# Value products of attention in longer runs, and gate and up by slices of the input, in a two-layer hybrid trunk

## The chip, the cores and the metric

The kernel runs on one core of one Trainium2 chip. The time is that of one launch on the device, in microseconds (us): 2272.66 us, the median of three runs that lie between 2272.47 and 2272.93 us. The profile is one further execution of the same program, recorded by the hardware profiler.

## The reference

One sequence of 512 tokens with 1024 features passes through two decoder layers. Each layer has three sub-layers, a feed-forward network (FFN), a token mixer and a second FFN, and each sub-layer is wrapped in the same way:

```python
def sandwich(x, fn, pre_g, post_g, shift, scale, gate, res_w):
    hn = rmsnorm(x, pre_g) * (1 + scale[:, None, :]) + shift[:, None, :]
    y = rmsnorm(fn(hn), post_g)
    return x + res_w * gate[:, None, :] * y

def swiglu(h, w_gate, w_up, w_down):          # FFN, inner width 2816
    return (jax.nn.silu(h @ w_gate) * (h @ w_up)) @ w_down
```

The mixer of layer 0 is multi-head latent attention (MLA): 16 heads, causal, in blocks of 128 queries. The core of it:

```python
s = jnp.einsum('bhqd,bhkd->bhqk', qi, kt) * scale     # masked: key position <= query position
p = jax.nn.softmax(s, axis=-1)
return jnp.einsum('bhqk,bhkd->bhqd', p, vt)           # the value products
```

The mixer of layer 1 is dilated attention (DIL): 16 heads of 64, each in three groups with dilation 1, 4 and 16 and a window, with a relative-position bias. The groups' outputs are added with weights from a softmax over their log-sum-exps:

```python
proj = (h @ w_in).reshape(B, S, N_GROUPS, 3, DIL_HEADS, DIL_HEAD_DIM)     # q, k, v of three groups
...
alpha = jax.nn.softmax(jnp.stack(lses, axis=0), axis=0)
o = jnp.sum(alpha[..., None] * jnp.stack(outs, axis=0), axis=0)
return o.reshape(B, S, DIL_WIDTH) @ w_o
```

All of it is in float32.

## The kernel before, in words

**Products.** Every product with a weight is three TensorE matmuls (`mm3`, lines 143, 144 and 145 of the profile): weight and input are split into a high and a low part, and high by high, high by low and low by high are added up in one PSUM bank. The high part of a weight is made by ScalarE (ACT, line 128, tile `whi`, 128x1024), the low part by VectorE (DVE, line 130, tile `wlo`, in two halves). Both come from a ring: six slots for `whi`, six for `wlo`, five for the raw weights that SyncE's queue (SP) loads. A slot is free when the last matmul that reads it has ended. PSUM has eight banks: four with the tag `mm` for products and scores, taken in turn, and four with the tag `aux` for transposes and value products.

**Stages.** The six sub-layers run one after the other: FFN, MLA, FFN, FFN, DIL, FFN. In the profile MLA's attention lies at about 447 to 590 us and DIL's at about 1396 to 1880 us, the FFNs before, between and behind.

**FFN.** Its 22 slices of 128 inner columns are in four groups of 5, 6, 5 and 6. `head` computes one slice: 24 matmuls for gate into one bank, 24 for up into a second (`gate_up_mm`), then `silu` on ACT (L567), the product on DVE (L569) and its split (L570, L572). After a group's last slice `down` multiplies the group with its slices of w_down.

**MLA.** `attend(c, i)` handles a pair of heads c and a block i of queries in three steps: `score` (L862), `turn`, which transposes the softmax's output on TensorE (L890) and copies it to SBUF, and `weigh`, the value products (L904). A value product uses 64 columns of the array (the profile's 128*64), one head in the upper and one in the lower half. A `Pipe` with a lag of 2 sets score of block i beside turn of an earlier and weigh of a still earlier block; products for the next heads (`BESIDE`) are put in between.

**DIL.** `rest` goes through 7 pairs p; in each it computes the nine projections of pair p+1 in the order (0, 1, 3, 4, 6, 7, 2, 5, 8), place n = 0 to 8. `tile` is one projection: 24 matmuls into one `mm` bank, which ACT then copies out (L1055) in one piece, or in four where group 2 needs another order of tokens (n = 4 and n = 5). Beside the projections stand `scores(p, n)` at n = 0 to 3 (L1090, two `mm` banks each, 64 rows of the array), `exps(p)` at n = 4 (48 exponentials on ACT, L1155), and `mix(p, step)`: `turn` (transposes, L1210, and copies) and `weigh` (value products, L1235, 128*64 again). Steps 0, 1 and 2 stand at n = 6, 7 and 8, steps 3 and 4 in the next pair at n = 0 and 1. The transposes at L1065 are those of the value projections.

**Order.** Apart from SP at the start and TensorE and DVE in DIL's last part, no order is written out: a list scheduler takes the program in the order of the code with its own costs and gives each engine a fixed list of instructions, which the engine works off in that order. So an edit of the code on TensorE can move instructions on the other engines.

Of the kernel before, what the change touches and what calls it, by code (L numbers as in the profile page):

```python
# [520 lines left out]
class Ffn:  # L521
# [19 lines left out]
    def gate_up_mm(self, ft, lo, hi, banks, ks):  # L541
        t = self.t
        if ft not in self.w:
            self.gate_up_load(ft)
        for g in range(2):
            for k in ks:
                t.mm3(
                    banks[g],
                    [x[:, k, :] for x in self.w[ft][g]],
                    [x[k][:, lo:hi] for x in t.h],  # L550
                    k == 0,
                    k == KT - 1,
                )
# [25 lines left out]
    def products(self, b, q, i, d, js):  # L579
        m = GROUPS[q][1]  # L580
        for j in js:
            self.t.mm3(
                b,
                [x[j][:, i * P : (i + 1) * P] for x in self.g[q]],
                [x[:, d * SEQ : (d + 1) * SEQ] for x in self.wd[q][j]],
                j == 0,
                j == m - 1,
            )
# [24 lines left out]
    def rest(self):  # L613
        t = self.t
        last = len(GROUPS) - 1
        for q, (at, n) in enumerate(GROUPS):
            if q == last - 1:
                t.gates(self)
            for ft in range(max(at, START if t.first is self else HEAD), at + n):
                self.head(ft, 0, SEQ)  # L620
                t.pump(3 if t.first is self else 2)
            for i in range(TT if q < last else 0):
                self.down(q, i)
# [76 lines left out]
class Mla(Mixer):  # L700
# [148 lines left out]
    def attend(self, c, i, pipe):  # L849
        t, nc = self.t, self.t.nc  # L850
        sc = 96.0**-0.5
        if i == 0:
            self.st = t.tmp.tile([P, 4, 6], F32, tag="st", name="st", bufs=3), {}
        st, box = self.st
        q, k = self.q[c], self.k[c]

        def score(i):
            n = (i + 1) * P
            box[i] = []
            for e in range(2):  # L860
                s = t.bank()[:, :n]
                nc.tensor.matmul(s, q[e][0:96, i * P : n], k[e][0:96, :n], start=True, stop=True)  # L862
                p = (t.t("u", UB) if i % 2 else t.t("sq", SB))[:, :n]
                nm, z = st[:, i, e : e + 1], st[:, i, 2 + e : 3 + e]
                nc.vector.tensor_tensor_reduce(
                    p, s, self.mask[:, SEQ - n :], -sc, 3e38, ALU.add, ALU.min, accum_out=nm
                )
                nc.scalar.activation(p, p, AF.Exp, bias=nm, scale=-1.0, accum_out=z)
                box[i].append(p)
            r = st[:, i, 4:6]  # L870
            nc.vector.reciprocal(r, st[:, i, 2:4])
            p = box[i]
            nc.vector.tensor_scalar(p[0], p[0], r[:, 0:1], None, ALU.mult)
            nc.scalar.activation(p[1], p[1], AF.Copy, scale=r[:, 1:2])

        def turn(i):
            n = (i + 1) * P
            tag = "gg" if i % 2 else "silu"
            ps = [t.bank("aux")]
            ys = [t.t(tag)]  # L880
            if i < 2:
                ps.append(ps[0][:, n:])
                ys.append(ys[0][:, n:])
            else:
                ps.append(t.bank("aux"))
                ys.append(t.t(tag))
            for e in range(2):
                for j in range(i + 1):
                    r = slice(j * P, (j + 1) * P)
                    nc.tensor.transpose(ps[e][:, r], box[i][e][:, r], t.ident)  # L890
            if i < 2:
                nc.vector.tensor_copy(ys[0][:, : 2 * n], ps[0][:, : 2 * n])
            else:
                nc.scalar.activation(ys[0][:, :n], ps[0][:, :n], AF.Copy)
                nc.vector.tensor_copy(ys[1][:, :n], ps[1][:, :n])
            box[i] = ys

        def weigh(i):
            if i == 0:
                box["o"] = t.bank("aux")  # L900
            for j in range(i + 1):
                for e in range(2):
                    h = 2 * c + e
                    nc.tensor.matmul(  # L904
                        box["o"][64 * e : 64 * e + 64, i * P : (i + 1) * P],
                        self.v[j, h // 8][:, (h % 8) * 64 : (h % 8) * 64 + 64],
                        box[i][e][:, j * P : (j + 1) * P],
                        start=i == j == 0,
                        stop=i == j == 3,
                        skip_group_check=True,  # L910
                    )
            if i == 3:
                self.put_o(box["o"])

        pipe.push(i, score, turn, weigh)

    def rest(self):
# [25 lines left out]
class Dil(Mixer):  # L943
# [302 lines left out]
            self.of.append(x)  # L1246

    def mix(self, p, step):
        if step < 4:
            self.turn(p, step)  # L1250
        if step:
            self.weigh(p, step - 1)

    def rest(self):
        t = self.t
        t.gates(self)
        self.of = []
        self.tables()
        for u in self.ORDER[6:]:
            self.tile(0, u, 0, SEQ)  # L1260
        for p in range(7):
            for n, u in enumerate(self.ORDER):
                if n < 4:
                    self.scores(p, n)
                if n < 2 and p:
                    self.mix(p - 1, 3 + n)
                if n == 4:
                    self.exps(p)
                if n >= 6:
                    self.mix(p, n - 6)  # L1270
                if p == 6 and n == 8:
                    self.scores(7, 0)
                self.tile(p + 1, u, 0, SEQ)
        self.later()
        self.scores(7, 1)
        for x in self.of[:PART]:
            self.put_o(x)
        self.mix(6, 3)
        t.new_y()
        for j in range(PART):  # L1280
            self.out_weights(j)
        self.scores(7, 2)
        self.mix(6, 4)
        self.scores(7, 3)
        for x in self.of[PART:]:
            self.put_o(x)
        self.exps(7)
        order = (2, 0, 1, 3)
        with t.tc.manual_schedule(engines={PE, DVE}):
            for n in range(6):  # L1290
                self.part(n)
            for n, step in enumerate(order):
                self.turn(7, step)
                if n:
                    self.weigh(7, order[n - 1], order[0], order[-1])
                if n in (0, 1):
                    self.part(6 + n)
            self.norm_out(self.pairs[7])
            self.weigh(7, order[-1], order[0], order[-1])
        self.put_o(self.of[-1])  # L1300
# [115 lines left out]
```

## Time and profile before

| | |
|---|---|
| median of three runs | 2272.66 us (2272.47 to 2272.93) |
| profiled execution | 2273.08 us |
| its span, first to last instruction | 2271.3 us |
| TensorE (PE) busy | 2240.5 us, 99% |
| VectorE (DVE) busy | 1203.6 us, 53% |
| ScalarE (ACT) busy | 861.3 us, 38% |
| GpSimd (POOL) busy | 105.2 us, 5% |
| granted TensorE clock, mean | 0.999 |

A line of the profile names engine, source line, operation, and the tiles as out<-in, with buffer numbers left out. In a timeline a row is a start, a duration, and a count (x8) of like instructions in succession. Matmuls overlap: one begins before the other ends, so the distance of two starts, not the duration, says what a matmul takes of TensorE's time. A bracket at a row's end is the time for which the engine stood idle before it, with what ended this wait. Value products and scores stand in the trace with two records for each matmul of the code, so x16 there is x8 in a list of the order.

### The profile page before, as it was taken

What the parts mean: (1) busy time and instruction counts of PE and PEld (TensorE: products, weight loads), DVE (VectorE), ACT (ScalarE), POOL (GpSimd) and SP (SyncE); (2) the same over time, 40 slices, a digit from 0 to 9 for tenths busy, and PEclk for the clock granted to TensorE, in tenths of its full rate; (3) what the DMA queues carried; (4) which work ended last, traced back from release to release, by engine and by line L of the source; (5) the groups of instructions that cost most, each with busy time, mean ns of one, the idle gap of its engine ahead of it and who ended that gap; (6) DMA issues with size and microseconds to landing.
All of it is one profiled execution on the core that took longest, in us unless ns stands there. A gap on an engine that the chain in (4) does not pass through costs nothing. (4 is left out here: it accounts for less than half of the span.)

```text
span 2271.3 us, 30190 instructions
## 1 busy us (share of the span) xinstructions
PE 2240.5 (99%) x11422; PEld 1851.4 (82%) x11422; DVE 1203.6 (53%) x2712; ACT 861.3 (38%) x1752; POOL 105.2 (5%) x143
## 2 busy tenths in 40 slices
PE   7999999999999999999999999999999999999998
PEld 5888888877898888898888888778878878888887
DVE  7666566677655366474554473334434367243344
ACT  4422135577633132353222352444344346332232
POOL 0000001210110000020000010000000002000000
PEclk9999999999999999999999999999999999999999
DMA  8575662311255365344653523333333332243231
GB/s 307 163 249 180 187 232 68 100 48 57 76 171 180 93 213 173 106 140 127 191 174 114 156 93 105 80 96 87 81 93 87 89 79 80 75 130 100 76 111 38
DMA packets 121224, 284.04 MB, mean 125 GB/s; under 512 B 44130, under 2 KB 48501, under 8 KB 121078
## 3 DMA queue, kind: packets, MB, share of 16 engines
q1 hardware_dynamic: 121078, 282.11, 40.8%
q8 instruction: 89, 1.46, 0.3%
q14 instruction: 57, 0.47, 0.1%
HBM read 279.67 MB, written 2.39 MB: 124 GB/s over the span
## 5 line engine op out<-in xcount | busy, mean ns | idle before, releaser
L143 PE MATMUL mm<-s,whi 128*128 128x512 f32 (+1 forms) x2116 | 796.9, 377 | 3.5 <-ACT whi L128 2.4
L144 PE MATMUL mm<-s,whi 128*128 128x512 f32 (+1 forms) x2116 | 790.9, 374 | 0.0
L145 PE MATMUL mm<-s,wlo 128*128 128x512 f32 (+1 forms) x2116 | 790.5, 374 | 0.0
L128 ACT ACTIVATE whi<-raw 128x1024 fp32r<-128x1024 f32 (+1 forms) x356 | 369.7, 1053 | 962.2 <-PE mm L144 446.6
L130 DVE TENSOR_TENSOR wlo<-raw,whi 128x512 fp32r<-128x512 f32 (+1 forms) x712 | 465.6, 693 | 397.8 <-ACT whi L128 393.8
L143 PEld LDWEIGHTS mm<-s,whi 128*128 128x128 f32 x2116 | 398.7, 188 | 83.4 <-issue 7.0
L145 PEld LDWEIGHTS mm<-s,wlo 128*128 128x128 f32 x2116 | 398.7, 188 | 70.9
L144 PEld LDWEIGHTS mm<-s,whi 128*128 128x128 f32 x2116 | 398.9, 188 | 68.1
L143 PE MATMUL mm<-whi,s 128*128 128x512 f32 x848 | 332.4, 392 | 1.8 <-ACT s L694 1.1
L144 PE MATMUL mm<-wlo,s 128*128 128x512 f32 x848 | 330.4, 390 | 0.0
L145 PE MATMUL mm<-whi,s 128*128 128x512 f32 x848 | 330.1, 390 | 0.0
L165 DVE CUSTOM_DVE_ANT_0 raw<-raw,cs 128x1024 f32<-128x1024 f32 x130 | 159.9, 1234 | 117.7 <-DMA raw<-w_mod 117.2
L143 PEld LDWEIGHTS mm<-whi,s 128*128 128x128 f32 x848 | 159.2, 188 | 36.3 <-issue 2.5
L145 PEld LDWEIGHTS mm<-whi,s 128*128 128x128 f32 x848 | 159.2, 188 | 33.4 <-issue 0.3
L144 PEld LDWEIGHTS mm<-wlo,s 128*128 128x128 f32 x848 | 159.3, 188 | 32.6 <-issue 0.3
L569 DVE TENSOR_TENSOR gg<-silu,mm 128x512 f32<-128x512 f32 (+1 forms) x95 | 60.3, 635 | 171.5 <-PE mm L145 168.3
L459 DVE TENSOR_TENSOR s<-mm,s 128x512 f32<-128x512 f32 x112 | 76.5, 689 | 125.8 <-PE mm L145 125.6
L318 POOL TENSOR_TENSOR mv<-mv,mhalf 128x1 f32<-128x1 f32 x48 | 36.0, 752 | 1498.0 <-DVE mv L317 1495.5
L570 ACT ACTIVATE s<-gg 128x512 fp32r<-128x512 f32 (+1 forms) x97 | 57.4, 591 | 62.0 <-DVE gg L569 62.0
L567 ACT ACTIVATE silu<-mm 128x512 f32<-128x512 f32 (+1 forms) x95 | 51.5, 543 | 31.9 <-PE mm L145 31.9
L1055 ACT ACTIVATE s<-mm 128x512 f32<-128x512 f32 (+3 forms) x156 | 46.2, 373 | 34.8 <-PE mm L145 34.8
L463 ACT ACTIVATE s<-mm 128x512 f32<-128x512 f32 x40 | 23.8, 595 | 85.8 <-PE mm L145 85.5
(168 smaller groups left out, 1737.3 us busy)
## 6 DMA issues: line engine op xcount, KB each, us to landing
raw<-w_gu SPq DMA_DIRECT2D x168, 512.0 KB, 4.3
raw<-w_mod SPq DMA_DIRECT2D x130, 512.0 KB, 4.8
raw<-w_down SPq DMA_DIRECT2D x88, 512.0 KB, 4.3
raw<-dil_in SPq DMA_DIRECT2D x70, 512.0 KB, 3.6
s<-w_mod SPq DMA_DIRECT2D x28, 256.0 KB, 6.3
raw<-w_gu SPq DMA_DIRECT2D x16, 256.0 KB, 3.6
raw<-mla_o SPq DMA_DIRECT2D x8, 512.0 KB, 3.7
raw<-dil_o SPq DMA_DIRECT2D x8, 512.0 KB, 3.6
```

Source lines behind the costliest of these rows:

```text
L128: self.nc.scalar.activation(hi, raw, AF.Copy)
L130: self.nc.vector.tensor_tensor(lo[:, r], raw[:, r], f(hi[:, r]), ALU.subtract)
L143: mm(out, w[0], m[0], start=first, stop=False)
L144: mm(out, w[0], m[1], start=False, stop=False)
L145: mm(out, w[1], m[0], start=False, stop=last)
L165: nc.vector.tensor_tensor_reduce(raw, raw, self.cs, 1.0, 0.0, ALU.mult, ALU.add, accum_out=t[:, 0:1])
L318: nc.gpsimd.tensor_tensor(v[:, 1:2], v[:, 0:1], self.mhalf[:, 0:1], ALU.pow)
L459: nc.vector.tensor_tensor(y, b, y, ALU.add)
L567: nc.scalar.activation(s, banks[0], AF.Silu)
L569: nc.vector.tensor_tensor(v, s, banks[1], ALU.mult)
L570: nc.scalar.activation(ghi, v, AF.Copy)
L1055: nc.scalar.activation(out, src, AF.Copy)
```

## The change

Three edits. `gate_up_mm` loops over the input's slices outside and over gate and up inside, so that its matmuls alternate between the two banks. In MLA the value products of blocks 0 and 1, and of blocks 2 and 3, are set together. In DIL `weigh` of steps 0 and 1 is issued at step 2 and that of steps 2 and 3 at step 4, ahead of the transposes of that step, and the two calls of `mix` for the former pair stand before `scores(p, 0)` and behind `scores(p, 1)`.

```diff
@@ Ffn.gate_up_mm
-        for g in range(2):
-            for k in ks:
+        for k in ks:
+            for g in range(2):
                 t.mm3(
                     banks[g],
@@ Mla.attend
         def weigh(i):
             if i == 0:
                 box["o"] = t.bank("aux")
+            elif i % 2:
+                for q in (i - 1, i):
+                    products(q)
+            if i == 3:
+                self.put_o(box["o"])
+
+        def products(i):
             for j in range(i + 1):
                 for e in range(2):
                     h = 2 * c + e
...
-            if i == 3:
-                self.put_o(box["o"])
@@ Dil.mix
     def mix(self, p, step):
+        if step in (2, 4):
+            for n in (step - 2, step - 1):
+                self.weigh(p, n)
         if step < 4:
             self.turn(p, step)
-        if step:
-            self.weigh(p, step - 1)
@@ Dil.rest
             for n, u in enumerate(self.ORDER):
+                if n == 0 and p:
+                    self.mix(p - 1, 3)
                 if n < 4:
                     self.scores(p, n)
-                if n < 2 and p:
-                    self.mix(p - 1, 3 + n)
+                if n == 1 and p:
+                    self.mix(p - 1, 4)
```

With it the lines move: L904 becomes L911, and in DIL L1055 becomes L1060, L1065 L1070, L1090 L1095, L1155 L1160, L1210 L1215 and L1235 L1240.

**TensorE in MLA.** The rows are TensorE's, from the transposes of one block to the next product; L862 are scores, L890 transposes, `aux<-silu,s` and `aux<-gg,s` the value products of even and odd blocks. Before:

```order
L862 MATMUL mm<-s 128x384 x2
L890 MATMUL aux<-ident,sq 128x128 x2
L904 MATMUL aux<-gg,s 64x128 x8
L143 MATMUL mm<-s,whi 128x512
...
L862 MATMUL mm<-s 128x512 x2
L890 MATMUL aux<-ident,u 128x128 x4
L904 MATMUL aux<-silu,s 64x128 x2
L143 MATMUL mm<-whi,s 128x512
```

After the change:

```order
L862 MATMUL mm<-s 128x384 x2
L890 MATMUL aux<-ident,sq 128x128 x2
L911 MATMUL aux<-silu,s 64x128 x6
L911 MATMUL aux<-gg,s 64x128 x8
L143 MATMUL mm<-whi,s 128x512
...
L862 MATMUL mm<-s 128x512 x2
L890 MATMUL aux<-ident,u 128x128 x4
L143 MATMUL mm<-whi,s 128x512
```

Two runs of value products are now one. Over MLA there were 32 separate runs and there are 18.

**TensorE in DIL, from place n = 7 to n = 8 of a pair.** Here with the buffers' numbers: `mm_14061` before and `mm_14056` after is the bank of the projection at n = 7, `mm_14120` that at n = 8. Before:

```order
L145 MATMUL mm_14061<-s_11065,wlo_14056 128x512
L1235 MATMUL aux_14048<-gg_14036,s_13544 64x256
L1235 MATMUL aux_14048<-gg_14042,s_13544 64x256
L1235 MATMUL aux_14048<-gg_14036,s_13544 64x128
L1235 MATMUL aux_14048<-gg_14042,s_13544 64x128
L143 MATMUL mm_14120<-s_11058,whi_14114 128x512
L144 MATMUL mm_14120<-s_11066,whi_14114 128x512
```

After the change:

```order
L145 MATMUL mm_14056<-s_11065,wlo_14051 128x512
L143 MATMUL mm_14120<-s_11058,whi_14114 128x512
L144 MATMUL mm_14120<-s_11066,whi_14114 128x512
L145 MATMUL mm_14120<-s_11058,wlo_14115 128x512
L143 MATMUL mm_14120<-s_11059,whi_14114 128x512
L144 MATMUL mm_14120<-s_11067,whi_14114 128x512
L1070 MATMUL aux_14082<-ident_75,s_14009 128x128 x4
L1240 MATMUL aux_14089<-silu_13988,s_13539 64x256
```

The value products between the two projections are gone; they stand behind the next transposes of a value projection. In all DIL has 32 runs of value products before and 18 after.

**ScalarE in DIL, the same pair.** The rows begin with the last exponentials of the pair. `mm_13922` is the bank of n = 4, `mm_13959` that of n = 5, `mm_14010` of n = 6; the four `whi` slots named are those of later projections. Before:

```order
L1155 ACTIVATE u_13804,dz_13625<-u_13804,y4_13830 128x128 x4
L128 ACTIVATE whi_14317<-raw_14315 128x1024
L128 ACTIVATE whi_14389<-raw_14387 128x1024
L1055 ACTIVATE s_13921<-mm_13922 128x128 x4
L1055 ACTIVATE s_13958<-mm_13959 128x128 x4
L1055 ACTIVATE s_14009<-mm_14010 128x512
L1055 ACTIVATE s_14060<-mm_14061 128x512
L128 ACTIVATE whi_14464<-raw_14462 128x1024
```

After the change:

```order
L1160 ACTIVATE u_13804,dz_13629<-u_13804,y4_13830 128x128 x4
L128 ACTIVATE whi_14317<-raw_14315 128x1024
L128 ACTIVATE whi_14389<-raw_14387 128x1024
L128 ACTIVATE whi_14464<-raw_14462 128x1024
L1060 ACTIVATE s_13921<-mm_13922 128x128 x4
L1060 ACTIVATE s_13958<-mm_13959 128x128 x4
L1060 ACTIVATE s_14009<-mm_14010 128x512
L1060 ACTIVATE s_14055<-mm_14056 128x512
```

The third conversion (`whi_14464`) stands ahead of ten copies instead of behind them. It is so in pairs p = 1 to 6; in pair p = 0 three conversions stand ahead of the copies before and after the change.

## Rows read from the trace of the kernel before

**Rows 1.** The page's first part: busy time, share of the span and instructions.

```profile
PE 2240.5 (99%) x11422; PEld 1851.4 (82%) x11422; DVE 1203.6 (53%) x2712; ACT 861.3 (38%) x1752; POOL 105.2 (5%) x143
```

**Rows 2.** Waits of TensorE: line, releaser, us in total, times, longest.

```profile
PE mm L143 <- ACT s L306: 3.8, 6, 1.2
```

**Rows 3.** Timeline of TensorE in MLA: start, duration, line, tiles, count.

```profile
500.88 1.09 PE L904 MATMUL aux<-gg,s 128*64 128x128 f32 x16
501.90 0.50 PE L143 MATMUL mm<-s,whi 128*128 128x512 f32 x1
...
505.79 0.60 PE L890 MATMUL aux<-ident,u 128*128 128x128 f32 x4
506.32 0.44 PE L904 MATMUL aux<-silu,s 128*64 128x128 f32 x4
506.69 0.50 PE L143 MATMUL mm<-whi,s 128*128 128x512 f32 x1
507.03 0.40 PE L144 MATMUL mm<-wlo,s 128*128 128x512 f32 x1
```

**Rows 4.** Timeline of TensorE late in DIL, transposes directly ahead of products.

```profile
1855.22 1.04 PE L1210 MATMUL aux<-ident,u 128*128 128x128 f32 x8
...
1856.32 0.40 PE L144 MATMUL mm<-wlo,s 128*128 128x512 f32 x1
```

**Rows 5.** Timeline of TensorE in DIL, pair p = 1, n = 6 to 8.

```profile
1508.22 0.82 PE L1210 MATMUL aux<-ident,sq 128*128 128x128 f32 x6
1508.97 1.08 PE L1235 MATMUL aux<-silu,s 128*64 128x256 f32 x8
...
1510.33 0.40 PE L144 MATMUL mm<-s,whi 128*128 128x512 f32 x1
...
1515.37 0.39 PE L145 MATMUL mm<-s,wlo 128*128 128x512 f32 x1
1515.69 0.87 PE L1235 MATMUL aux<-gg,s 128*64 128x256 f32 x8
1516.49 0.50 PE L143 MATMUL mm<-s,whi 128*128 128x512 f32 x1
1516.83 0.40 PE L144 MATMUL mm<-s,whi 128*128 128x512 f32 x1
```

**Rows 6.** Timeline of TensorE, value products directly behind scores.

```profile
1524.80 1.09 PE L1235 MATMUL aux<-silu,s 128*64 128x128 f32 x16
1525.83 0.50 PE L143 MATMUL mm<-s,whi 128*128 128x512 f32 x1
```

**Rows 7.** Timeline of TensorE in DIL, pair p = 0, n = 7 to 8.

```profile
1452.12 0.39 PE L145 MATMUL mm<-s,wlo 128*128 128x512 f32 x1
1452.44 0.87 PE L1235 MATMUL aux<-gg,s 128*64 128x256 f32 x8
1454.16 0.50 PE L143 MATMUL mm<-s,whi 128*128 128x512 f32 x1 [0.85 <-ACT s L1055]
1454.49 0.39 PE L144 MATMUL mm<-s,whi 128*128 128x512 f32 x1
```

**Rows 8.** Timeline of ScalarE in the same stretch, pair p = 0.

```profile
1452.38 1.06 ACT L128 ACTIVATE whi<-raw 128x1024 fp32r<-128x1024 f32 x1 [6.34 <-PE mm L144]
1453.34 2.42 ACT L1055 ACTIVATE s<-mm 128x128 f32<-128x128 f32 x10
```

**Rows 9.** Timeline of ScalarE in pair p = 1.

```profile
1509.20 1.93 ACT L1055 ACTIVATE s<-mm 128x128 f32<-128x128 f32 x9
...
1516.35 1.05 ACT L128 ACTIVATE whi<-raw 128x1024 fp32r<-128x1024 f32 x1
```

**Rows 10.** Timeline of VectorE where an FFN's group of slices begins.

```profile
1159.74 2.50 DVE L130 TENSOR_TENSOR wlo<-raw,whi 128x512 fp32r<-128x512 f32 x4 [1.08 <-ACT whi L128]
```

**Rows 11.** Timeline of TensorE at the same place.

```profile
1161.85 0.39 PE L143 MATMUL mm<-s,whi 128*128 128x512 f32 x1
...
1162.98 0.39 PE L145 MATMUL mm<-s,wlo 128*128 128x512 f32 x1
```

## The prediction

> **What bounds the kernel now.** I read the page's busy times first: TensorE is busy for 99% of the span, VectorE for 53%, ScalarE for 38% [rows 1]. So time is saved only where TensorE's own list of instructions becomes shorter, and lost wherever TensorE is made to wait. Next came its waits: where an FFN takes over its input, six waits for ACT's L306 add up to 3.8 us [rows 2]; none of the list is for a value product's operand. Then the timeline of TensorE at the places that the change touches, looking at the distance of starts: five steps of a 512-column product from 1161.85 to 1162.98 us are 1.13 us, 0.226 us each [rows 11]. Last the same stretches on ACT, since TensorE in DIL depends on ACT's copies for free banks.
>
> **What a run of value products costs beside its own work.** In MLA four transposes, four value products and a product follow one another: from the first transpose (505.79) to the second product (507.03) it is 1.24 us [rows 3]. Without the value products, eight transposes take 1.10 us to the same point, 1855.22 to 1856.32 [rows 4]. A transpose takes 0.11 us: six need 0.75 (1508.22 to 1508.97) [rows 5], four 0.53 (505.79 to 506.32) [rows 3], and two more make 0.22. So four transposes without value products take 1.10 - 0.44 = 0.66 us. The value products' own work: 16 take 1.02 us to the next product (500.88 to 501.90), four take 0.37 (506.32 to 506.69), so 0.65/12 = 0.054 us each and 0.22 for four [rows 3]. What is left is 1.24 - 0.66 - 0.22 = 0.36 us for one separate run: 0.15 of it between its first record and the product behind, 0.1 in the slower first step of that product (0.34 instead of 0.23), the rest at its entry.
>
> *A page against these rows.* The Trainium skill, TensorE: Matmul & The Clock Gate, section Step-by-step: what each phase is for, says that one matmul's drain runs beside the next one's fill, so that matmuls in succession are spaced by their columns alone. By that a run's ends would cost nothing and merging runs would save nothing. The trace differs here: 0.34 us behind a run against 0.226 us elsewhere.
>
> **MLA.** 32 separate runs become 18: 14 x 0.36 = 5.0 us saved. The work of the products is the same. What a merged run costs is not shown for a run of two tiles; the lower bound of the saving is the 0.15 us inside alone, 14 x 0.15 = 2.1 us, the upper one 0.36 each. I take the upper one, since entry and exit both go with the run. The even block's value products now come later, so their `silu` buffer comes free later, and the copies of the next block wait on it on DVE; behind them are transposes and scores of a next block, which the pipe's lag of two keeps off TensorE's path. I put nothing for it. If that cover were gone, TensorE would lose up to the length of a run of 16 for each pair of heads, 8 x 1.02 = 8 us [rows 3]; only the range's upper part holds some of that.
>
> **DIL, the runs.** In each of seven pairs the runs of steps 0 and 1 become one: one overhead less, 0.36 us. The rows agree: from the transposes at 1508.22 to the second product at 1510.33 it is 2.11 us, of which six transposes and two products are 1.10 - 0.22 = 0.88; from the last product ahead (1515.37) to the second one behind (1516.83) 1.46, of which two steps are 0.46; 2.23 us in all for both runs [rows 5]. Steps 2 and 3 stand next to score runs in both versions. There 16 value products take 1.03 us until the product (1524.80 to 1525.83), of which 16 x 0.054 = 0.87 is work; 0.16 is saved when two such runs become one [rows 6]. Together 0.52 x 7 = 3.6 us. Bounds: 0.15 and 0.72 for both, 1.1 to 5.0 us.
>
> **DIL, ACT's list.** This is where I expect the gain to go. Moving the value products from n = 7 to n = 8 changes the scheduler's list for ACT: in pairs 1 to 6 a third weight conversion (L128) stands ahead of the ten copies (L1055) that free the banks of n = 4 to 7. That conversion's slot is the one that the projection at n = 7 reads, six conversions earlier, so it cannot begin before the last matmul of n = 7 that reads it. And the first matmul at n = 8 needs the bank of n = 4, the fourth back, whose copies stand behind that conversion. So TensorE stands still for a conversion and four copies.
>
> The trace shows this very order once, in pair 0. ACT waits 6.34 us for a product L144, begins the conversion at 1452.38, and the copies at 1453.34 [rows 8]. TensorE's last product of n = 7 begins at 1452.12, so n = 8 could begin at 1452.12 + 0.23 = 1452.35; it begins at 1454.16, with 0.85 us of it shown as a wait for L1055, and its next step takes 0.33 instead of 0.23 [rows 7]. Part of it is covered there by value products. Without them the loss is 1454.16 - 1452.35 + 0.10 = 1.91 us. In pair 1, where only two conversions stand ahead, the copies begin at 1509.20 [rows 9], 7.3 us before n = 8 needs its bank at 1516.49, and the eight products take 0.80 us, with no wait [rows 5]; the third conversion comes at 1516.35, when the copies are done [rows 9].
>
> After the change all seven pairs have the order of pair 0, and the value products no longer stand in the gap: 7 x 1.91 = 13.4 us. Pair 0 lost already 1454.16 - 1452.44 - 0.80 = 0.92 us [rows 5, 7]. The change adds 13.4 - 0.9 = 12.5 us. Behind the waiting conversion on ACT stand the ten copies, 2.42 us in all [rows 8]; who waits for these is TensorE at n = 8, and five products later the value projection's transposes. The timeline of pair 0 shows no bracket ahead of these, so I add none. Bounds: below, the shown wait alone, 7 x 0.85 - 0.85 = 5.1 us, or nothing at all if the bank were free; above, a wait for all ten copies, 7 x (0.03 + 0.96 + 2.42 + 0.10) - 0.9 = 23.7 us.
>
> **FFN.** The matmuls are the same in number and form, and gate and up use two banks as before; at 0.226 us a step it makes no difference which comes first. What changes is when up's weight is needed: after three matmuls of a slice, not after 24. Where a group begins, DVE makes four low halves from 1159.74 in 2.50 us, so the third, up's first, is there by 1161.6 [rows 10]; TensorE starts the slice at 1161.85 and needs that half five steps later, at 1162.98 [rows 11]. 1.3 us are left, so nothing is lost. In return silu and the product for a slice come both at its end; the next slice's 48 matmuls (10.8 us at 0.226) hide them. Where an FFN takes over its input, TensorE waits for the input's slices and not for the order of gate and up [rows 2]; both orders end at the arrival of the last one. I put 0, with 2 us either way for these places: about half of the 3.8 us.
>
> **The sum.** -5.0 - 3.6 + 12.5 = +3.9 us. The profiled execution took 2273.08 us, 1.8 us beyond its span, and is 0.4 us above the median; the same execution after the change would take 2277.0 us, and the median 2272.66 + 3.9 = about 2276.5 us.
>
> **Rivals.**
> *ACT does not hold TensorE* (faster). If the slot or the bank were free in time in pairs 1 to 6, as before, only the runs count: 2272.66 - 5.0 - 3.6 = 2264.1 us. For it: before the change six of seven pairs show no wait. Against it: pair 0, where the same three conversions stand ahead and the wait is there. Chance 0.14.
> *Half of it holds.* If TensorE loses only the 0.95 us that pair 0 shows as a wait and slow step: 7 x 0.95 - 0.92 = 5.7, so 2272.66 - 8.6 + 5.7 = 2269.8 us. For it: something else of TensorE's list might stand in the gap, as value products did. Against it: the list shows only the products of n = 8 there. Chance 0.08.
> *The FFN pays for up's weight* (slower). One mechanism: at the twelve places where a group follows another within an FFN, up's first low half comes too late. It decides once more than 1.3 us of other work stands ahead of that half on DVE; three further halves of 0.62 us (1.88) would leave a wait of 0.5 us, 12 x 0.5 = 6 us, and 2282.5 us with the rest. For it: the weights of w_down are made by the same engine in the same stretch. Against it: the margin of 1.3 us [rows 10, 11]. Chance 0.09.
> *Merging saves nothing* (slower): the runs' ends cost TensorE no time that it could use otherwise, and only the waits count, 2272.66 + 12.5 = 2285.2 us. Against it: the 0.36 us in rows 3 and 4. Chance 0.07. The rule cited above, of the Trainium skill, TensorE: Matmul & The Clock Gate, section Step-by-step: what each phase is for, would have it so.
>
> **How the numbers follow.** My forecast has 0.62, with a range of its own of 2273 to 2280 us. A measurement of this kernel can tell about 0.2%, 4.5 us, from no change, so the limit lies at 2277.2 us, close above the forecast; of its 0.62 I put 0.38 below the limit and 0.24 above. Faster: 0.14, the first rival. Same: 0.38 + 0.08 = 0.46. Slower: 0.24 + 0.09 + 0.07 = 0.40. For 8 in 10 the range reaches from 2265, near the first rival, to 2283 us, past the FFN's.
>
> **What would show it.** Right: waits of TensorE for the moved copies (L1060) at n = 8 of every pair, of about 1.8 us each and 12 to 13 us in all; ACT's third conversion beginning at the end of n = 7 in each pair; MLA's attention shorter by about 5 us; DIL longer by about 9; the FFNs equal within 2. Wrong: no such wait, or one of under a microsecond; value products in long runs whose next product still takes as much per run; a new wait for `wlo` (L130) in an FFN, or for a copy in MLA.

## The result, and the profile after

The changed kernel takes 2280.99 us (median of six runs, 2278.15 to 2284.72) where the kernel before took 2273.32 us in its six (2272.47 to 2275.56). The ratio is 1.0032, with a 95% interval of 1.0022 to 1.0042: about 7.3 us longer, where I had forecast 3.9 us. The profiled execution of after took 2280.28 us, its span is 2278.5 us against 2271.3.

TensorE is busy for as long as before (2239.4 us against 2240.5); it waits more. Its waits after (line, releaser, us in total, times, longest):

```profile
PE mm L143 <- ACT s L1060: 9.9, 6, 1.6
PE mm L377 <- DVE s L371: 5.3, 4, 3.3
PE mm L143 <- ACT s L306: 2.4, 5, 0.7
...
PE mm L1095 <- ACT s L1060: 1.6, 1, 1.6
```

Before there was one wait for these copies, of 0.85 us [rows 7]; now there are seven, of about 1.6 us each, 11.5 us in all. The seventh is put down to L1095, since in the last pair scores stand ahead of the projection at n = 8. The wait for L306 was 3.8 us [rows 2].

Here is the place in pair p = 1 that answers to rows 5 and 9, TensorE's timeline first (start, duration, line, tiles, count, idle time and its releaser):

```profile
1512.04 0.39 PE L145 MATMUL mm<-s,wlo 128*128 128x512 f32 x1
1514.07 0.50 PE L143 MATMUL mm<-s,whi 128*128 128x512 f32 x1 [1.65 <-ACT s L1060]
1514.40 0.39 PE L144 MATMUL mm<-s,whi 128*128 128x512 f32 x1
...
1515.34 0.60 PE L1070 MATMUL aux<-ident,s 128*128 128x128 f32 x4
1515.87 1.08 PE L1240 MATMUL aux<-silu,s 128*64 128x256 f32 x8
1516.78 0.82 PE L1240 MATMUL aux<-gg,s 128*64 128x256 f32 x8
```

and ACT's:

```profile
1512.30 1.06 ACT L128 ACTIVATE whi<-raw 128x1024 fp32r<-128x1024 f32 x1 [5.11 <-PE mm L144]
1513.26 2.42 ACT L1060 ACTIVATE s<-mm 128x128 f32<-128x128 f32 x10
```

ACT stands idle for 5.11 us, until the last product L144 of n = 7 frees a slot, then converts, then copies; TensorE goes on 0.81 us after the copies began, when four of them are done. It is the pattern of pair 0 before [rows 7, 8], with nothing left to cover it: 1514.07 - 1512.04 - 0.23 = 1.80 us, and 0.10 in the next step, 1.90 us for the pair.

In MLA the merged run looks like this, with the transposes that now go straight into a product behind it:

```profile
499.66 0.38 PE L890 MATMUL aux<-ident,sq 128*128 128x128 f32 x2
499.97 0.88 PE L911 MATMUL aux<-silu,s 128*64 128x128 f32 x12
500.68 1.04 PE L911 MATMUL aux<-gg,s 128*64 128x128 f32 x16
501.65 0.50 PE L143 MATMUL mm<-s,whi 128*128 128x512 f32 x1
...
505.57 0.60 PE L890 MATMUL aux<-ident,u 128*128 128x128 f32 x4
505.93 0.48 PE L143 MATMUL mm<-whi,s 128*128 128x512 f32 x1
506.24 0.40 PE L144 MATMUL mm<-wlo,s 128*128 128x512 f32 x1
```

In records of the trace (two for each value product, as in the prediction), 28 take 1.68 us to the next product. Apart, 16 take 1.02 us and 12, at 0.054 a piece more than four, 0.80 [rows 3], so the join saves 0.14 us inside, and the run has one entry instead of two. From four transposes to the second product it is 506.24 - 505.57 = 0.67 us, as the prediction had worked out (0.66).

Where the time went, by the starts of the same instruction in both traces: the first scores of MLA (L862) come at 447.65 before and 447.93 after, +0.28 us; DIL's first value transposes (L1065, then L1070) at 1394.12 and 1391.67, -2.46; those of the last pair's n = 8 at 1835.24 and 1842.58, +7.34; the span ends +7.2. So DIL cost 9.8 us, and what lies between gained 2.7 and would have gained more but for the clock. Right behind MLA's first two waits (0.64 and 0.78 us, in both traces) TensorE of this execution ran at the lower clock. Products there, and the window's row (TensorE busy, ..., granted clock, DMA share, GB/s):

```profile
450.20 0.77 PE L143 MATMUL mm<-s,whi 128*128 128x512 f32 x1
450.76 0.63 PE L144 MATMUL mm<-s,whi 128*128 128x512 f32 x1
```

```profile
450.00:453.00 3.00, 3.00 (x10) 2.37 (x9) 1.34 (x8) 2.99 (x9) 0.30 (x1) 0.57 0.26 105
```

The steps take about 0.43 us instead of 0.23 up to 453.75, just ahead of the scores at 454.04. The distance to before grew from 0.28 to 1.86 us over this stretch, 1.58 us. From there to DIL it falls from +1.86 to -2.46: MLA's longer runs gained 4.3 us.

### The profile page after: what moved, and what is told of

Read it like the earlier page. It is cut to its first block, busy times and chain, and to the rows that moved or that the text cites. A ratio compares the mean times of both kernels' runs of the same rounds, so it can differ in the third digit from the quotient of the medians.

```text
span 2278.5 us, 30263 instructions
## 1 busy us (share of the span) xinstructions
PE 2239.4 (98%) x11422; PEld 1855.9 (81%) x11422; DVE 1197.8 (53%) x2712; ACT 849.6 (37%) x1752; POOL 108.4 (5%) x143
## 5 line engine op out<-in xcount | busy, mean ns | idle before, releaser
L144 PE MATMUL mm<-s,whi 128*128 128x512 f32 (+1 forms) x2116 | 791.7, 374 | 0.0
L130 DVE TENSOR_TENSOR wlo<-raw,whi 128x512 fp32r<-128x512 f32 (+1 forms) x712 | 467.8, 693 | 583.4 <-ACT whi L128 579.4
L144 PEld LDWEIGHTS mm<-s,whi 128*128 128x128 f32 x2116 | 399.8, 189 | 68.4
L144 PE MATMUL mm<-wlo,s 128*128 128x512 f32 x848 | 330.5, 390 | 0.0
L144 PEld LDWEIGHTS mm<-wlo,s 128*128 128x128 f32 x848 | 159.3, 188 | 32.8 <-issue 0.5
L144 PE MATMUL mm<-s 128*128 128x256 f32 (+1 forms) x176 | 53.3, 308 | 3.0 <-DVE s L307 2.1
L1160 ACT ACTIVATE u<-u,y 128x128 f32<-128x128 f32 x128 | 49.5, 388 | 15.6 <-DVE y L1141 15.6
```

Source lines behind the costliest of these rows:

```text
L130: self.nc.vector.tensor_tensor(lo[:, r], raw[:, r], f(hi[:, r]), ALU.subtract)
L144: mm(out, w[0], m[1], start=False, stop=False)
L1160: nc.scalar.activation(c, c, AF.Exp, bias=pair["top"][:, g, i, one], scale=-1.0, accum_out=pair["z"][:, g, i, one],)
```

## The experiments

Each kernel is compared with executions of the kernel before that ran beside it; their median was 2274.5 to 2274.6 us, and a ratio is to be read against that. The labels e1 to e10 stand for the kernels below. In code, "..." marks lines left out.

**One edit at a time.** MLA's edit alone on the kernel before (e1), its middle:

```diff
...
+            elif i % 2:
+                for q in (i - 1, i):
+                    products(q)
...
```

> Before, with the edit of MLA's value products alone. Theory (the parts add up: MLA's merged runs save, DIL's copies behind a third conversion cost): MLA's attention is shorter by the 4.3 us that the trace of after shows between its first scores after 454 us and DIL's start, to at most 5.0 us, so 2268 to 2269 us where before takes 2273. Rival (merging value products saves nothing of its own, MLA gained by another edit or by a lag made up): within 1 us of before. Rival on the clock (longer runs of value products bring stretches at the lower clock): the mean clock of some executions falls to 0.997 or less, and the time spreads over some us.

Measured: 2270.70 us (2270.09 to 2274.14), ratio 0.9984 [0.9975, 0.9993], some 3.6 us less, a little short of the 4.3 to 5.0 expected. By the trace, MLA's span from its first scores to the second product behind its last value product falls from 134.63 to 130.41 us, 4.2 us or 0.30 us for each of 14 runs, not 0.36. Both ends of a run are in it, some 2.1 us each. At its entry the first value product comes 0.20 us after the last transpose, where without a run a product comes after 0.03 and a score after 0.11; and what follows a run comes after 0.20 us, where inside a run the next value product comes after 0.05. Against it stand dearer entries of three runs that are left between products (0.28 us together). The rival that merging saves nothing has fallen. What the rival on the clock named was there in a small way: four of eleven executions have a mean of 0.997 (three of 21 of the kernel before), none below, and took 2270.74 to 2274.14 us, the others 2270.09 to 2270.74; it does not undo the gain.

FFN's edit alone (e2):

```diff
-        for g in range(2):
-            for k in ks:
+        for k in ks:
+            for g in range(2):
```

> Before, with gate and up alternating by slice alone. Theory: between 0 and +0.5 us, the trace of after stands 0.3 us behind at MLA's start and nothing is added in the later FFNs. Rival (up's weight, needed earlier, makes TensorE wait at the groups' starts): +2 us or more, with waits of TensorE for wlo (L130). Rival on the clock: executions at 0.997 or less.

Measured: 2273.94 us (2272.95 to 2276.76), ratio 0.9999 [0.9990, 1.0008]. Nothing, as forecast.

DIL's edit alone (e3; the two parts of the diff in `mix` and `rest`, of which the first is shown):

```diff
+        if step in (2, 4):
+            for n in (step - 2, step - 1):
+                self.weigh(p, n)
         if step < 4:
             self.turn(p, step)
-        if step:
-            self.weigh(p, step - 1)
...
```

> Before, with the edit of DIL alone. Theory: the waits for the copies (L1055) at n = 8 of seven pairs come back in full, about 1.6 us each in the list of waits; DIL is longer by 9 to 10 us, so 2282 to 2283 us where before takes 2273, and executions differ by some us, since a wait of this length may be followed by a stretch at the lower clock. Rival (the waits come from MLA or FFN running ahead, which shifts loads and conversions): less than 3 us, with the waits for the copies gone or short.

Measured: 2282.49 us (2281.86 to 2285.96), ratio 1.0040 [1.0027, 1.0052]. Its waits:

```profile
PE mm L143 <- ACT s L1055: 9.9, 6, 1.6
...
PE mm L1090 <- ACT s L1055: 1.6, 1, 1.6
```

To a tenth those of after. The loss is DIL's own, and the others do not cause it.

**What the wait is for.** First the copies of n = 4 alone were taken from ACT in the changed kernel (e4; u is the projection's number, 6 at n = 4, 7 at n = 5 and 2 at n = 6):

```diff
-            nc.scalar.activation(out, src, AF.Copy)
+            if u == 6 and p:
+                nc.vector.tensor_copy(out, src)
+            else:
+                nc.scalar.activation(out, src, AF.Copy)
```

> After, with one thing changed: in pairs 1 to 7 the projection at n = 4 is copied out of its bank by DVE instead of ACT, so that its bank no longer waits behind the third weight conversion on ACT; the lists of TensorE and ACT are otherwise the same but for the place of one product. Theory (head of the line on ACT): the waits at n = 8 go in all pairs, about 12.5 us come back and the time is before's less 8, some 2265 us. Rival (n = 8 waits for something else that comes as late, its own weight or the value products' place): the waits stay, now put down to another releaser, and the time stays within 3 us of after's 2281. Rival (DVE is late with the four copies): waits for DVE's copy of 0.5 to 1 us in each pair, 2270 to 2275 us. On the clock: if the dips follow the waits, the clock is as in before in every execution.

Measured: 2283.11 us (2278.63 to 2286.49), ratio 1.0036 [1.0023, 1.0049]: nothing came back. In its trace DVE has copied n = 4 in pair 1 long before, from 1510.90 on, and TensorE still waits for ACT until 1514.08:

```profile
PE mm L143 <- ACT s L1063: 9.9, 6, 1.6
...
PE mm L1098 <- ACT s L1063: 1.6, 1, 1.6
```

```profile
1510.90 0.83 DVE L1061 COPY s<-mm 128x128 f32<-128x128 f32 x4
```

The built program says why: banks are not simply taken in turn. With n = 4 on DVE the scheduler gave n = 8 the bank of n = 5, as it would if it expected that one to be free first (in the pair of the lists under The change, PSUM bank 6; in after it is bank 7, that of n = 4). Its four copies stand on ACT behind the same conversion. So this run did not take away what it meant to; the next one did (e5), with `u in (6, 7)`, n = 4 and n = 5 on DVE.

> After, with the projections at n = 4 and at n = 5 of pairs 1 to 7 copied out by DVE. In the run with n = 4 alone on DVE the program gave n = 8 the bank of n = 5, whose copies were still on ACT behind the third conversion; the waits stayed as they were. With both on DVE no bank that n = 8 can get waits for ACT. Theory (head of the line on ACT): the seven waits of 1.6 us go; about 12 us come back, and the time is some 7 us below before, 2266 to 2268 us where before takes 2273 to 2274. Rival (TensorE at n = 8 is bound by something else that comes as late, such as its weight or the next step on DVE): waits of like length with another releaser, within 3 us of after. Rival (only the number of ACT's copies matters, not the conversion ahead): half comes back. On the clock: the mean is 0.997 to 0.999 in every execution as in before, and the spread falls to 4 us.

Measured: 2276.67 us (2274.10 to 2277.17), ratio 1.0008 [0.9999, 1.0017]: about 5.5 us below after by the ratios, where 12 were expected. All seven waits at n = 8 for ACT are gone, 11.5 us, but others have come, 7.0 us:

```profile
PE aux L1073 <- ACT s L1063: 4.4, 6, 0.8
...
PE mm L143 <- DVE s L1061: 2.6, 1, 2.6
```

L1073 are the transposes of a value projection, in this kernel three products into n = 8 (five in after). They read the copy of n = 6, and that is the next instruction on ACT behind the conversion. The third rival (half comes back) had the number, but not the mechanism. The one wait of 2.6 us for DVE, in pair 0, goes back to the same conversion: the low half of that weight (L130) needs it and stands on DVE ahead of the copies. DVE's rows there, before TensorE goes on at 1451.26:

```profile
1449.62 0.69 DVE L130 TENSOR_TENSOR wlo<-raw,whi 128x512 fp32r<-128x512 f32 x1 [2.47 <-ACT whi L128]
1450.23 1.67 DVE L1061 COPY s<-mm 128x128 f32<-128x128 f32 x8
```

With n = 6 on DVE too, `u in (6, 7, 2)` (e9):

> After, with the projections at n = 4, 5 and 6 of pairs 1 to 7 copied out by DVE. With n = 4 and 5 on DVE the waits at n = 8 went, but TensorE then waited 0.8 us in six pairs, 4.4 us in all, for ACT's copy of n = 6, which the value projection's transposes read five products later, and which is the next one behind the third conversion; and once 2.6 us for DVE. Theory (the blocked head of ACT's queue holds whatever stands behind it): with this copy on DVE too, the 4.4 us go, the wait for DVE stays; 2271 to 2273 us where the kernel with two copies on DVE took 2276.7. Rival (the remaining loss is DVE's load): no gain, waits for DVE of the same sum.

Measured: 2269.94 us (2267.18 to 2271.21), ratio 0.9980 [0.9971, 0.9989]; the waits for ACT are gone, those for DVE are left:

```profile
PE mm L143 <- DVE s L1061: 3.4, 2, 2.6
```

So it is the conversion that holds back whatever stands behind it, and each wait removed showed the next one in line. 2269.94 is below the 2271 expected. This step is not a clean one: in e9 the list also has the transposes eight products into n = 8 and not three, so not all of the gain need be the moved copy's.

The same kernel as e5 with FFN as before (e8), to see FFN's edit beside fewer waits:

> As after with both projections on DVE, but FFN as before. Theory: FFN's edit is worth nothing, so within 1 us of the kernel with both projections on DVE, 2266 to 2268 us. Rival (alternating gate and up helps or harms once the waits are gone): a difference of 2 us or more.

Measured: 2275.74 us (2274.77 to 2276.64), ratio 1.0005 [0.9997, 1.0014], as e5 within its interval. The 2266 to 2268 us named were what was expected of e5, and fell with that.

**The suspected wait made longer.** After, with n = 4 copied twice on ACT (e7):

```diff
-            nc.scalar.activation(out, src, AF.Copy)
+            for _ in range(2 if u == 6 and p else 1):
+                nc.scalar.activation(out, src, AF.Copy)
```

> After, with the suspected wait made longer: in pairs 1 to 7 ACT copies the projection at n = 4 out of its bank twice, four small copies more behind the third conversion. Theory: each of the seven waits grows by four copies, about 0.8 us, to 2.4 us, 17 us in all: 5 to 6 us longer than after by the waits alone, 2284 us in an execution without further dips of the clock, and more executions with a mean of 0.996 or less. Rival (the wait is for the conversion or for another copy, not for those of n = 4): waits as in after, no longer time.

Measured: 2293.53 us (2289.48 to 2294.99), ratio 1.0081 [1.0068, 1.0095]. The waits:

```profile
PE mm L143 <- ACT s L1061: 17.0, 6, 2.8
...
PE mm L1096 <- ACT s L1061: 2.8, 1, 2.8
```

19.8 us, 1.2 more in each pair, not 0.8: in this kernel the scheduler gave n = 8 the bank of n = 5, as with n = 4 on DVE, and set the copies of both among each other, so that the copy that frees the bank is the eleventh and not the eighth. The time rose by some 11 us over after's by the ratios: more than the 8.3 us of waits. The rest goes with the clock: three of the four executions have a mean of 0.995 or 0.996, and the one at 0.998 took 2289.48 us, 9.2 more than after's at 0.998. Behind the wait at n = 8 of one pair (TensorE could have gone on at 1773.70 and did at 1776.69) the windows show, with the granted clock third from the end:

```profile
1772.00:1776.00 4.00, 1.86 (x9) 1.20 (x7) 1.40 (x4) 2.27 (x10) 0.00 (x0) 0.99 0.29 100
1776.00:1779.00 3.00, 2.31 (x7) 1.71 (x7) 0.11 (x1) 1.79 (x7) 0.00 (x0) 0.50 0.70 201
1779.00:1782.00 3.00, 3.00 (x17) 1.72 (x16) 0.69 (x1) 0.00 (x0) 0.00 (x0) 0.50 0.73 175
```

Half the clock, 1.2 instead of 2.4 GHz, for the six microseconds after the wait; the same follows the wait in the last pair, at 1845 us. Behind the other five waits of this trace, as long as these, the clock stays up.

**The order on ACT undone, the longer runs kept.** Products of steps 0 and 1 issued at step 1, behind its transposes, instead of at step 2; on the kernel before with MLA's edit and DIL's, FFN as before (e6; the diff is against after and leaves out FFN's lines):

```diff
     def mix(self, p, step):
-        if step in (2, 4):
-            for n in (step - 2, step - 1):
+        if step == 4:
+            for n in (2, 3):
                 self.weigh(p, n)
         if step < 4:
             self.turn(p, step)
+        if step == 1:
+            for n in (0, 1):
+                self.weigh(p, n)
```

> Before, with MLA's edit and with DIL's longer runs, but the run of steps 0 and 1 is issued at n = 7, behind the transposes of step 1, and FFN as before. By the order TensorE then has one run of both between n = 7 and n = 8, and ACT has two conversions ahead of the copies in every pair. Theory: no wait at n = 8, and both savings: 3.6 us of MLA and 0.36 + 0.16 us a pair in DIL, 3.6 us, and 0.9 us of pair 0: 2265 to 2267 us where before takes 2273 to 2274. Rival (the longer runs in DIL save nothing, all that DIL's edit does is the waits): 2270 us, as with MLA's edit alone.

Measured: 2266.82 us (2264.35 to 2267.56), ratio 0.9964 [0.9952, 0.9977], no wait for the copies. On one point the expectation erred: TensorE does not have these products between n = 7 and n = 8 but between n = 6 and n = 7, where before had those of step 0 alone. The same edit on after, with all three parts of the change in it (e10):

> After with one change: the products of steps 0 and 1 are issued at step 1 behind its transposes, not at step 2. All three edits are in it, the runs are as long as in after, and between n = 7 and n = 8 TensorE has products of projections alone, as in after; but ACT has two conversions ahead of the copies. Theory (ACT's order alone makes the waits): no wait at n = 8 and 2265 to 2268 us, within 1 us of the same order with FFN as before (2266.8). Rival (value products missing between n = 7 and n = 8 leave the wait uncovered): waits of 1.6 us as in after, 2278 us or more. Rival (FFN's edit does harm beside the others): 2 us or more above 2266.8.

Measured: 2264.28 us (2264.15 to 2266.33), ratio 0.9958 [0.9945, 0.9970], the fastest kernel of this study, 9.5 us below before by the ratio and 2.5 below e6's median, where at most 1 was expected (by the ratios 1.4 us, within both intervals). Between n = 7 (its last full step at 1510.42) and the transposes at 1511.56 TensorE has products of projections alone,

```profile
1510.19 0.39 PE L144 MATMUL mm<-s,whi 128*128 128x512 f32 x1
1510.42 0.39 PE L145 MATMUL mm<-s,wlo 128*128 128x512 f32 x1
1510.64 0.39 PE L143 MATMUL mm<-s,whi 128*128 128x512 f32 x1
...
1511.56 0.60 PE L1070 MATMUL aux<-ident,s 128*128 128x128 f32 x4
```

with no bracket at 1510.64, since ACT made the copies 7 us earlier and holds the third conversion back:

```profile
1503.64 1.93 ACT L1060 ACTIVATE s<-mm 128x128 f32<-128x128 f32 x9
1510.90 0.60 ACT L1060 ACTIVATE s<-mm 128x512 f32<-128x512 f32 x1 [5.34 <-PE mm L145]
1511.40 1.05 ACT L128 ACTIVATE whi<-raw 128x1024 fp32r<-128x1024 f32 x1
```

This settles cover against order: without value products there to cover anything, the wait is absent as long as two conversions and not three stand ahead.

## Why the prediction was right, and where its sizes were off

- *The mechanism.* Right in place, cause and number: seven waits at n = 8 for the copies behind a third conversion, each like pair 0 before. The wide range (2265 to 2283 us) held 2281, and the sign was right; but the likeliest case, a change too small to tell, with 0.46, was not what came. The 0.40 for slower was. The forecast's own range (2273 to 2280) was missed by 1 us, and of the times named that of the FFN rival, 2282.5, lies nearest; it is e2, and no wait for `wlo` at the groups' starts, that rules it out.
- *The sizes.* The terms that were off, below, all missed towards a longer time, so nothing cancelled in the sum.
- *A pair's loss, taken as 1.91 us.* After against e10, which differ in this, DIL's distance grows from 1.59 us at its start to 15.88 at the last pair: 14.3 us, 2.04 us a pair, 0.9 us above the 13.4 of the sum. In pair 1 the wait and the step behind it make 1.90; what is above that lies in the steps further behind, some hundredths of a us each, and in the last pair, where scores follow the wait.
- *DIL's longer runs, taken as 3.6 us, with 0.9 of pair 0.* e10 against before: from -4.05 to -8.54 us over DIL, 4.5 us, the sum of the two. The prediction gives 2.23 us for two runs and says that this agrees with 0.36 saved, without working it out; e10's rows in pair 1 do:

```profile
1502.66 0.82 PE L1215 MATMUL aux<-ident,sq 128*128 128x128 f32 x6
1503.41 1.08 PE L1240 MATMUL aux<-silu,s 128*64 128x256 f32 x8
...
1505.41 0.40 PE L144 MATMUL mm<-s,whi 128*128 128x512 f32 x1
```

  1505.41 - 1502.66 = 2.75, less the same 0.88 for transposes and two products, is 1.87 us for both runs in one, 0.36 below 2.23.
- *MLA, taken as 5.0 us.* 4.2 us in the trace of the edit alone, 4.3 in after's. The term was mis-sized: 0.36 us for a run was read where transposes and products stand at both sides, and not each of the 14 runs stood so. The upper bound should not have been the value taken. The parts of the 0.36 were misread too: the first step of a product is nearly as slow straight behind transposes (505.93 to 506.24, 0.31 us) as behind a run (0.34), so that step is 0.03 of it and not 0.1, and the entry is more; the difference as a whole is not touched by this.
- *FFN.* 0 forecast, -0.2 measured (interval -2.3 to +1.8 us); no wait for `wlo` at the groups' starts, where the third low half is again made ahead. At the start of the kernel after is 0.28 us behind, within what I had left to the range.
- *The clock.* No term of the sum had it, and by subtraction it is the largest part of what was missing. The shortest executions of both kernels, 2278.15 and 2272.47, lie 5.7 us apart, near the 3.9 + 0.9 + 0.8 + 0.3 = 5.9 us that the terms above make of the forecast; the medians lie 7.7 us apart. Two of after's six executions have a mean clock of 0.995 and 0.996 and took 2284.72 and 2283.47 us, while those at 0.999 took 2278.15 and 2279.82. Of the 21 executions of before in the first comparison none is below 0.997, nor one of the kernels without these waits (e1, e5, e6, e8, e9, e10); of the run with n = 4 on DVE two of five are, of that with longer waits three of four; of DIL's edit alone, which has the waits, none of five, though two at 0.997 took 3 us more than the others. That waits of about 1.65 us bring the lower clock is not shown: in the traces of after, e3 and e4 none of the 21 is followed by it (granted clock 1.00 from 1448 to 1846 us), and what e7's trace shows is for waits of 2.8 us. After's own profiled execution has two stretches at 0.50 between 31 and 2276 us, one in MLA and one at 1908 us, where the last FFN takes over its input, both behind waits that before has too. So for the slower executions of after the cause of their lower mean clock is open.
- *The Trainium skill's rule.* The rule that the prediction cites (the Trainium skill, TensorE: Matmul & The Clock Gate, section Step-by-step: what each phase is for), of matmuls spaced by their columns alone, would have made merging worthless; e1 and e6 show that it saves time in both attentions.

## What to carry to other kernels

A fixed list per engine means that an edit for one engine has to be read on the others: here six conversions that moved ahead of sixty copies on ACT took back more than three times what DIL's longer runs gave on TensorE. Look for an instruction that waits for a resource freed late, and ask what is queued behind it and who needs that. When a copy is moved to another engine, check which buffer the waiting instruction then gets; a scheduler that chooses buffers by its own forecast may hand it the next blocked one.

## What was not expected of the hardware

The lower clock behind single waits in a TensorE stream that is otherwise 98% busy: granted clock 0.50 for the six microseconds after two of e7's waits of 2.8 us, about 3 us lost each time, which doubles the price of such a wait where it happens. It follows some waits and not others, and length alone does not decide. A wait of 2.6 us in pair 0 (for DVE) was followed by 0.50 in e5 and e8, and not in e9; the seven of 1.65 us in after by none; but MLA's first two, of 0.64 and 0.78 us, were followed by it in after, e2, e4, e7 and e9, and not in before, e1, e3, e5, e6, e8 and e10. What decides was not tried.
